# The end of the attention in a hybrid block: two modulation tiles, four norms and the first row of the output projection written earlier

## The chip, the cores and the metric

The kernel runs on one core of a Trainium2 chip. The metric is device time in microseconds (us); the median of several runs counts. A core has five engines with queues of their own: TensorE (PE: matmuls and transposes into PSUM), VectorE (DVE), ScalarE (ACT), GpSimd (POOL) and SyncE (SP), which here only issues DMA transfers. Each engine takes its instructions in the order in which they are queued.

## What is computed (the reference, cut)

One layer of a diffusion backbone: 512 latent tokens of width 2048 and 256 context tokens that serve only as extra keys and values.

```python
mod_l = silu(c) @ w_ada + b_ada            # 6 x 2048 modulation values
sh_a, sc_a, gt_a, sh_f, sc_f, gt_f = split(mod_l, 6)
h = rms_norm(x, g_mix_norm) * (1 + sc_a) + sh_a
qa, kva, kr, cb, cc, ch = split_projection(h @ w_in)
att  = softmax(q @ k.T * scale) @ v        # 8 heads of 128, keys: latent + context
conv = cb * (dwconv3(cc * ch) + bias)      # 8 groups of 128
mix  = rms_norm per group of 128 of [att, conv]
x = x + gt_a * (mix @ w_out)
x = x + gt_f * conv_ffn(rms_norm(x) * (1 + sc_f) + sh_f)
return rms_norm(x, g_final)
```

The change lies between `softmax(...) @ v` and `mix @ w_out`.

## The kernel before, in words

Arrays lie with features on the 128 partitions and tokens along the free axis, so a tile is 128x512 float32 (`t2`, a pool of 58 such tiles). A float32 product is made of three fp32r matmuls (`mm3`, L187 to L189): each operand is split into a rounded high part (a copy on ScalarE) and the rest (a subtraction on VectorE): high x high, high x low, low x high.

**The attention loop** (from L838) has 32 steps n: 8 heads with 4 blocks of 128 query tokens. Step n does the softmax of step n+1 (`softmax`, L745 and L748: the minimum `mn` on VectorE, then the exponential `p` on ScalarE), the six transposes of its own `p` (`transposes`, L761) with their split into `pth` (ScalarE, L764) and `ptl` (VectorE, L765), and the scores of step n+2 (`scores`, L730 to L734). At every even step the product of p and v for the half head that ended two steps before follows (`attend`: 18 matmuls `po`, and a copy to `o`, L777). Each eighth step sums the squares of two heads (`merge_sum`, L785 to L793: matmuls `gs`, a power on GpSimd); two steps later `merge` lays the factor out (`gb`, L299) and scales the heads (L803). The last product, `attend(7, 1)`, and the last `merge_sum(3)` come after the loop.

Between these, the loop carries other work:

- **Late modulation tiles.** 56 of the 96 rows of the modulation are made as dot products on VectorE: `late_load` (L145 on SyncE's queue, 1 MB into one of two buffers `raw`) brings a tile `ra`, and `late_dot(0)` and `late_dot(1)` (L263, 128x1024 each) multiply it, one step after the load. `keep` pins each L263 behind the VectorE instruction that is traced just before it. In the projection the tiles are called `ada` and have four half buffers of their own; their room is that of the attention's `p`, `pth` and `ptl` tiles.
- **Late norms.** `late_bg` holds the norms of the 8 convolution groups (`gn_apply`: four transposes `gb<-io,gn` at L299, then L374 on VectorE). Four are done before the loop, the other four in steps 25, 27, 29 and 31.
- **First weights of the output projection.** In steps 29 and 30 two loads `ofr` (768 KB each, L145) bring the weights of rows 0 to 3, into the same two `raw` buffers.

**The output projection** first makes 6 of its 16 output tiles at once: 16 rows k, each with 6 x 3 = 18 matmuls `of<-mx..` (`out_row`), for the convolution groups (k = 0 to 7) and then the heads (k = 8 to 15). `out_row` first splits its operand (`mx`, L337 and L338); the weights are split by `blocks` (`ofw`, L166 and L167, three splits of 128x512 for two rows). Rows 0 to 3 (`OUT_EARLY`) are written inside the attention's pools, the others after them, with `late_both` (two L263 and the next load) behind each row. Then come the other ten output tiles (`whole`), of which the last two are made in halves of 256 tokens (`ol0`, `ol1`), the residual (L980), the norm's sum of squares (`rms_steps`, tile `rs`) and the feed-forward part, which begins with matmuls `uf`.

**What sets the order.** Tile's scheduler orders each engine's queue: it takes what is ready first in its own estimate, and among that what stands first in the program. So a program line that moves changes a priority; only `keep` and `issue_after` force an order, and the latter only on the engine of the instruction that it names.

**PSUM** has eight banks of 128x512. In the attention, scores and other tiles share a pool; after it, `bank_of(i)` names banks, and `in_turn` deals them out. Before the change the last product and sum get banks 6 and 7, and the six output tiles banks 0 to 5.

Of the kernel before, what the change touches and what calls it, by code (L numbers as in the profile page):

```python
# [10 lines left out]
F32 = mybir.dt.float32  # L11
F32R = mybir.dt.float32r
AF = mybir.ActivationFunctionType
ALU = mybir.AluOpType
# [7 lines left out]
NK = D // P  # L22
# [9 lines left out]
G = 6  # L32
# [5 lines left out]
OUT_EARLY = 4  # L38
# [34 lines left out]
def block_kernel(ctx, tc, xt, ctxt, ctxn, c, c_ctx, w_ada, small, w_in, w_inc, w_q, w_kv, w_out,  # L73
# [3 lines left out]
    V, A, G_, PE, SP = nc.vector, nc.scalar, nc.gpsimd, nc.tensor, nc.sync  # L77
# [29 lines left out]
    one_bank = [None]  # L107
# [92 lines left out]
    bg, post, late_bg = deque(), [], []  # L200
# [70 lines left out]
    def late_load(ld):  # L271
        if late["t"] < late["end"]:
            late["raw"] = ld(late["t"])

    def late_both(ld=None):
        late_dot(0)
        late_dot(1)
        if ld is not None:
            late_load(ld)
# [120 lines left out]
    with ExitStack() as pa:  # L400
# [163 lines left out]
        for ci, (k0, n) in enumerate(zip(K0, KCH)):  # L564

            pss = first_banks(f"pf{ci}")
# [22 lines left out]
            for i, m in enumerate(ORDER[G:]):  # L589
                if i % per == 0:  # L590
                    k = min(per, len(ORDER) - G - i) * n
# [46 lines left out]
    with ExitStack() as pb:  # L638
# [112 lines left out]
        def transposes(st, pt):  # L751
            hd, tt = st
            half, b = tt // 2, tt % 2
            if b == 0:
                PT[hd, half] = [a_sb.tile([P, 6, 256], F32R, tag=f"pt{z}", bufs=2, name=f"pt{z}{hd}{half}") for z in "hl"]
            pth, ptl = PT[hd, half]
            bs = slice(b * P, (b + 1) * P)
            for u in range(2):
                tr = sml(f"t{hd}{tt}{u}")
                for kb in range(3):  # L760
                    PE.transpose(tr[:, kb * P:(kb + 1) * P], pt[:, (3 * u + kb) * P:(3 * u + kb + 1) * P], ident)  # L761
                trv = tr[:, :384].rearrange("p (k t) -> p k t", k=3)
                hi = pth[:, 3 * u:3 * u + 3, bs]
                A.copy(out=hi, in_=trv)  # L764
                V.tensor_tensor(out=ptl[:, 3 * u:3 * u + 3, bs], in0=trv, in1=hi.bitcast(F32), op=ALU.subtract)  # L765

        def attend(hd, half):
            pr, i = hd // 2, hd % 2
            pth, ptl = PT[hd, half]
            if half == 0:  # L770
                oo[hd] = t2([P, T], F32, f"o{hd}")
            po = sml(f"po{hd}{half}")
            for kb in range(6):
                c0 = (kb % 2) * 256 + i * P
                vh, vl = VV[pr, kb // 2]
                mm3(po[:, :256], (vh[:, c0:c0 + P], vl[:, c0:c0 + P]), (pth[:, kb], ptl[:, kb]), kb == 0, kb == 5)
            A.copy(out=oo[hd][:, half * 256:(half + 1) * 256], in_=po[:, :256])  # L777

        def merge_sum(pr):


            ps = sml(f"gs{pr}")
            for i in range(2):
                sq = tmp([P, T], F32, f"gq{pr}{i}")
                A.activation(sq, oo[2 * pr + i], AF.Square)  # L785
                for g in range(4):
                    PE.matmul(ps[:, i * 4 + g:i * 4 + g + 1], sq[:, g * P:(g + 1) * P], ones[:, 0:1], start=True, stop=True)
            d = den[pr]
            r = tiny(8, f"gr{pr}")
            V.tensor_tensor(out=d, in0=d, in1=d, op=ALU.mult)  # L790
            V.tensor_scalar(d, d, scalar1=EPS, scalar2=None, op0=ALU.mult)
            V.scalar_tensor_tensor(out=r, in0=ps[:, :8], scalar=1.0 / P, in1=d, op0=ALU.mult, op1=ALU.add)  # L792
            G_.tensor_tensor(out=r, in0=r, in1=half, op=ALU.pow)  # L793
            den[pr] = r

        def merge(pr):
            r = den[pr]
            for i in range(2):
                hd = 2 * pr + i
                pb_ = sml(f"gb{hd}")  # L800
                spread(pb_, r[:, 4 * i:4 * i + 4])
                o = oo[hd]
                V.scalar_tensor_tensor(out=o, in0=o, scalar=s("g_out", hd), in1=pb_, op0=ALU.mult, op1=ALU.mult)  # L803
                mixa[hd] = o
# [33 lines left out]
        for n, st in enumerate(steps):  # L838
            pr = st[0] // 2
            if n + 1 < len(steps):  # L840
                nxt_pt = softmax(steps[n + 1], ss[(n + 1) % 2])
            transposes(st, pt)
            pt = nxt_pt
            late_dot(0)
            if n + 2 < len(steps):
                ss[n % 2] = scores(steps[n + 2])
            if n % 2 == 0 and n:
                attend(*divmod(n // 2 - 1, 2))
                if n % 8 == 0:
                    merge_sum(n // 8 - 1)  # L850
            if n % 8 == 2 and n > 8:
                merge(n // 8 - 1)
            late_dot(1)
            if n > 24 and n % 2:
                deque(late_bg[4 + (n - 25) // 2], 0)

            at = n % 8
            if at == 0 and n and n < 24:
                fetch(pr + 1, 1)
            if pr < 3 and n:  # L860
                f, p_, i = pieces(pr + 1)[at]
                f(p_, i)
            if at < 2 and n < 24:
                fetch(pr + 1, 2 + at)
            elif at >= 2 and n < 29:
                late_load(ada_raw)
                if at == 6 and n < 16:
                    fetch(pr + 2, 0)
            if n in (29, 30):
                k = 2 * (n - 29)  # L870
                out_raw[k] = load(w_out_first[k // 2], 2 * G * P, f"ofr{k}")
            pump(2)

# [3 lines left out]
        def bank_of(i, nm):  # L877
            return p8.tile([P, 512], F32, tag=f"s{i}", bufs=1, name=nm)

        def in_turn(order):  # L880

            banks = deque(order)

            def f(nm):
                banks.rotate(-1)
                return bank_of(banks[-1], nm)

            return f


        for i in range(8):
            bank_of(i, f"bank{i}")
        one_bank[0] = in_turn((6, 7))
        attend(7, 1)
        merge_sum(3)
        pss = [bank_of(g, f"of{g}") for g in range(G)]
        mix = []

        def out_row(k, w):
            mix.append(hilo((mixc + mixa)[k], T, f"mx{k}"))  # L900
            row(pss, w[k % 2], mix[k], k)

        for k in range(OUT_EARLY):
            if k % 2 == 0:
                w = row_weights(w_out_first, k, "of", raw=out_raw[k])
            out_row(k, w)
        merge(3)
        drain()


    ph0.close()
    one_bank[0] = in_turn((6, 7, 0, 1, 2, 3, 4, 5))
    f_sb = ph1.enter_context(tc.tile_pool(name="fsb", bufs=1, side="right", reuse_waits="tile"))
    spare["w"] = f_sb, 2, 3
    g_sb = ph1.enter_context(tc.tile_pool(name="gsb", bufs=1, side="right", reuse_waits="tile"))
# [72 lines left out]
    for k in range(OUT_EARLY, NK):  # L988
        if k % 2 == 0:
            w = row_weights(w_out_first, k, "of")  # L990
        out_row(k, w)
        late_both(ada_spare if k % 4 < 3 or k == NK - 1 else None)
    for m in range(NK - 2):
        x_tile(m)
        residual(m, pss[m] if m < G else whole([load(w_out[m - G], D, f"o{m}r")], mix, f"o{m}", ld=ada_spare, often=m > 9))
# [166 lines left out]
    pss = [bank_of(i, f"uf{g}") for g, i in enumerate((2, 3, 4, 5, 1, 0))]  # L1162
# [508 lines left out]
```

## Time and profile before

| | us |
|---|---|
| median of 3 runs | 2132.49 (2132.07 to 2137.19) |
| the profiled execution | 2139.37 |
| its span in the trace | 2137.6 |
| PE busy | 2091.0 |
| DVE busy | 1826.5 |
| ACT busy | 1047.5 |

The profile is of one execution. A line of a timeline gives the start, the duration, engine, line of the kernel, operation, output<-inputs, and in brackets the idle time before it with what released it. Matmuls are pipelined, so their durations overlap: the distance between starts is what one costs. A line of waits gives who waited for whom, and the total, the count and the longest. "PEclk" is the share of full clock that was granted to TensorE.

In this execution the attention's loop runs from about 447 to 619 us, the first rows of the projection begin at 628, and the projection ends near 813.

### The profile page before, as it was taken

The page shows a single profiled execution, that of the slowest core. Times are in us where ns is not written, and L with a number is a line of the kernel's source. Part 1 is how long each engine was busy: PE and PEld are TensorE (multiplying, and loading weights), DVE is VectorE, ACT ScalarE, POOL GpSimd, SP SyncE. Part 2 cuts the span into 40 slices and gives each one's busy share as a digit, 9 for nine tenths or more (in the row PEclk, how much of TensorE's full clock was granted, in tenths as well). Part 3 has the DMA queues.
Part 4 walks back from the last instruction along what each step waited for, and adds up shares of the span by engine and source line. Part 5 has one row for each costly group of instructions (what it writes and reads, how often), then busy time and mean ns, then how long its engine had stood idle before and what let it go on. Part 6 is the DMA issues. An engine that isn't in the chain of part 4 may idle for free.

```text
span 2137.6 us, 35318 instructions
## 1 busy us (share of the span) xinstructions
PE 2091.0 (98%) x13268; PEld 1881.8 (88%) x13268; DVE 1826.5 (85%) x3024; ACT 1047.5 (49%) x1715; POOL 117.2 (5%) x144
## 2 busy tenths in 40 slices
PE   7999999999999999999999999999999999999997
PEld 4688788888988888999999999999999889999997
DVE  7998987778896989898999999999999658888887
ACT  5533333555552337565555555555655433333445
POOL 0000000000000100011000000000000000000000
PEclk9999999999999999999999999999999999999999
DMA  8989886334459986577788888788888989878684
GB/s 331 343 279 329 276 275 195 126 128 152 166 188 353 348 283 220 142 217 207 230 238 232 233 233 244 224 234 234 235 229 229 362 306 307 250 231 239 197 236 134
DMA packets 170177, 513.75 MB, mean 240 GB/s; under 512 B 18963, under 2 KB 23315, under 8 KB 164371
## 3 DMA queue, kind: packets, MB, share of 16 engines
q1 hardware_dynamic: 133364, 418.14, 57.7%
q0 software_dynamic: 17408, 59.25, 14.1%
q10 hardware_dynamic: 19232, 34.09, 4.2%
q8 instruction: 104, 1.70, 0.3%
q14 instruction: 69, 0.56, 0.1%
HBM read 464.22 MB, written 46.14 MB: 239 GB/s over the span
## 4 chain that ended last, share of the span: by engine, by line
PE 90%; DVE 4%; DMA 3%; ACT 2%; issue 1%; SPq 0%; DVEq 0%; ACTq 0%; POOLq 0%
PE pp L187 4%; PE pp L189 4%; PE pp L188 4%; PE d L187 1%; PE o L187 1%; PE d L188 1%; PE o L188 1%; PE d L189 1%; PE o L189 1%; PE uf L187 1%; PE uf L189 1%; PE uf L188 1%; PE of L187 1%; PE of L188 1%; PE of L189 1%; PE pf L188 1%
## 5 line engine op out<-in xcount | busy, mean ns | idle before, releaser
L1151 POOL DMA_DIRECT2D u_s<-in_w_up x80 | 68.6, 857 | 684.0 <-DMA u_s<-in_w_up 378.1
L263 DVE SCALAR_TENSOR_TENSOR ada<-ada,sv 128x1024 f32<-128x1024 f32 x68 | 82.1, 1220 | 11.4 <-DMA ada<-in_w_ada 11.2
L166 ACT CAST w_0h<-rw 128x512 fp32r<-128x512 f32 (+1 forms) x63 | 38.3, 618 | 108.3 <-PE pp L188 67.6
L241 DVE SCALAR_TENSOR_TENSOR ada<-ada,sv 128x1024 f32<-128x1024 f32 x64 | 77.6, 1220 | 2.2 <-DMA ada<-in_w_ada 2.1
L530 DVE SCALAR_TENSOR_TENSOR ada<-ada,svc 128x1024 f32<-128x1024 f32 x64 | 76.0, 1219 | 2.5 <-DMA ada<-in_w_ada 2.4
L167 DVE TENSOR_TENSOR w_0l<-rw,w_0h 128x512 fp32r<-128x512 f32 (+1 forms) x63 | 42.7, 683 | 22.8 <-ACT w_0h L166 22.6
L263 DVE SCALAR_TENSOR_TENSOR ra<-ra,sv 128x1024 f32<-128x1024 f32 x44 | 52.5, 1219 | 1.1 <-DMA ra<-in_w_ada 1.1
L1265 DVE TENSOR_TENSOR u<-u,u_s 128x1024 f32<-128x1024 f32 x40 | 48.8, 1220 | 0.7 <-DMA u_s<-in_w_up 0.5
L1266 DVE TENSOR_TENSOR u<-u,u 128x1024 f32<-128x1024 f32 x40 | 48.7, 1218 | 0.0
L793 POOL TENSOR_TENSOR gr<-gr,half 128x8 f32<-128x8 f32 x4 | 10.1, 2524 | 630.1 <-DVE gr L792 538.2
L764 ACT CAST pth<-t 128x384 fp32r<-128x384 f32 x64 | 28.6, 485 | 26.4 <-PE t L761 26.4
L1075 DVE TENSOR_TENSOR tp<-a,tp 128x256 fp32r<-128x256 f32 x90 | 37.7, 419 | 3.3 <-ACT tp L1074 3.3
L1074 ACT CAST tp<-a 128x256 fp32r<-128x256 f32 x90 | 35.7, 403 | 5.5 <-DMA yl6h<-y_d 4.2
L1038 ACT ACTIVATE g<-g 128x512 f32<-128x512 f32 x43 | 27.3, 634 | 18.3 <-DVE g L1032 18.0
L541 DVE TENSOR_TENSOR acc<-acc,pp 128x512 f32<-128x512 f32 x50 | 34.1, 683 | 2.1 <-PE pp L189 2.1
L765 DVE TENSOR_TENSOR ptl<-t,pth 128x384 fp32r<-128x384 f32 x64 | 33.2, 550 | 2.6 <-ACT pth L764 2.6
L745 DVE TENSOR_REDUCE mn<-s 128x1 f32<-128x768 f32 x32 | 30.4, 953 | 4.9 <-PE s L734 4.6
L1030 ACT ACTIVATE g<-cg,sm 128x512 f32<-128x512 f32 x40 | 32.6, 815 | 0.0
L1030 ACT ACTIVATE a<-ca,sm 128x512 f32<-128x512 f32 x40 | 32.1, 802 | 0.0
L748 ACT ACTIVATE p<-s,mn 128x768 f32<-128x768 f32 x32 | 29.3, 916 | 1.6 <-DVE mn L745 1.3
L1031 DVE SCALAR_TENSOR_TENSOR g<-cg,sm,g 128x511 f32<-128x511 f32 x40 | 29.8, 746 | 0.0
L1032 DVE SCALAR_TENSOR_TENSOR g<-cg,sm,g 128x511 f32<-128x511 f32 x40 | 29.8, 746 | 0.0
(10238 smaller groups left out, 8925.0 us busy)
## 6 DMA issues: line engine op xcount, KB each, us to landing
ada<-in_w_ada SPq DMA_DIRECT2D x196, 512.0 KB, 5.7
u<-in_w_up SPq DMA_DIRECT2D x120, 512.0 KB, 8.9
w<-t_d SPq DMA_DIRECT2D x161, 256.0 KB, 5.3
u_s<-in_w_up SPq DMA_DIRECT2D x80, 512.0 KB, 4.0
u_s<-in_w_up POOLq DMA_DIRECT2D x80, 512.0 KB, 9.6
t_d<-tp ACTq DMA_DIRECT2D x126, 256.0 KB, 5.9
v<-in_w_dnw SPq DMA_DIRECT2D x72, 384.0 KB, 5.1
ra<-in_w_ada SPq DMA_DIRECT2D x22, 1024.0 KB, 4.8
```

Of the source, the lines that this page charges most:

```text
L166: A.copy(out=hi[:, :n], in_=raw[:, a:a + n])
L167: V.tensor_tensor(out=lo[:, :n], in0=raw[:, a:a + n], in1=hi[:, :n].bitcast(F32), op=ALU.subtract)
L187: PE.matmul(ps, w[0], x[0], start=first, stop=False, skip_group_check=on_top)
L188: PE.matmul(ps, w[0], x[1], start=False, stop=False, skip_group_check=on_top)
L189: PE.matmul(ps, w[1], x[0], start=False, stop=last, skip_group_check=on_top)
L241: V.scalar_tensor_tensor(out=r, in0=r, scalar=1.0, in1=vec[:, i * 1024:(i + 1) * 1024], op0=ALU.mult, op1=ALU.mult, accum_out=col[:, i:i + 1])
L263: keep(V.scalar_tensor_tensor(out=r, in0=r, scalar=1.0, in1=svs[i], op0=ALU.mult, op1=ALU.mult, accum_out=lc[:, t % 4:t % 4 + 1] if i else ...
L530: keep(V.scalar_tensor_tensor(out=raw[q], in0=raw[q], scalar=1.0, in1=svc[:, q * 1024:(q + 1) * 1024], op0=ALU.mult, op1=ALU.mult, accum_o ...
L1030: A.activation(u, src, AF.Identity, bias=s("fb", m), scale=s("fw", 86 + m))
L1151: G_.dma_start(r[-1], src[more], accum_op=ALU.add)
L1265: V.tensor_tensor(out=a11, in0=a11, in1=s1, op=ALU.add)
L1266: V.tensor_tensor(out=a12, in0=a12, in1=a11, op=ALU.add)
```

## The change

1. The late norms are applied in steps 24, 25, 26 and 27 in place of 25, 27, 29 and 31.
2. The last three late tiles of the loop are loaded in steps 24, 25, 26 in place of 26, 27, 28, and multiplied in steps 25, 26, 27.
3. The weights `ofr` of rows 0 to 3 are loaded in steps 27 and 28 in place of 29 and 30.
4. Row 0 of the projection is written ahead of `attend(7, 1)` and `merge_sum(3)`, which follow between row 0 and row 1.
5. The banks: the last product and sum get 0 and 1, the six output tiles 4, 5, 6, 7, 2, 3; the tiles after them follow in the turn 0, 1, 4, 5, 6, 7, 2, 3.
6. The last `ptl` is remembered, and what `late_both` traces at row 4 is queued behind it with `issue_after`.

```diff
-                V.tensor_tensor(out=ptl[:, 3 * u:3 * u + 3, bs], in0=trv, in1=hi.bitcast(F32), op=ALU.subtract)
+                ptl_last[:] = [V.tensor_tensor(out=ptl[:, 3 * u:3 * u + 3, bs], in0=trv, in1=hi.bitcast(F32), op=ALU.subtract).ins]
+
+        ptl_last = []
...
-            if n > 24 and n % 2:
-                deque(late_bg[4 + (n - 25) // 2], 0)
+            if 24 <= n < 28:
+                deque(late_bg[4 + n - 24], 0)
...
-            elif at >= 2 and n < 29:
+            elif (at >= 2 or n >= 24) and n < 27:
                 late_load(ada_raw)
...
-            if n in (29, 30):
-                k = 2 * (n - 29)
+            if n in (27, 28):
+                k = 2 * (n - 27)
                 out_raw[k] = load(w_out_first[k // 2], 2 * G * P, f"ofr{k}")
...
-        one_bank[0] = in_turn((6, 7))
-        attend(7, 1)
-        merge_sum(3)
-        pss = [bank_of(g, f"of{g}") for g in range(G)]
+        one_bank[0] = in_turn((0, 1))
+        pss = [bank_of(b, f"of{b}") for b in (4, 5, 6, 7, 2, 3)]
...
             out_row(k, w)
+            if k == 0:
+                attend(7, 1)
+                merge_sum(3)
...
-    one_bank[0] = in_turn((6, 7, 0, 1, 2, 3, 4, 5))
+    one_bank[0] = in_turn((0, 1, 4, 5, 6, 7, 2, 3))
...
-        late_both(ada_spare if k % 4 < 3 or k == NK - 1 else None)
+        with tc.issue_after(ptl_last[0]) if k == OUT_EARLY else ExitStack():
+            late_both(ada_spare if k % 4 < 3 or k == NK - 1 else None)
```

## The prediction

> **What bounds the kernel now.** I read the page first (engine shares, chain of waits), then busy time by windows around the change, then the list of what TensorE waited for, then the timelines of TensorE, VectorE and SyncE's DMA queue over the same 40 us.
>
> ```profile
> span 2137.6 us, 35318 instructions
> ...
> PE 90%; DVE 4%; DMA 3%; ACT 2%; issue 1%; SPq 0%; DVEq 0%; ACTq 0%; POOLq 0%
> ```
>
> TensorE carries nine tenths of the chain that ended last, so a microsecond taken out of its waits is, at first, a microsecond of the span. In the windows the columns are the stretch, its length, busy time of PE, PEld, DVE, ACT, POOL, then granted clock, DMA share and GB/s:
>
> ```profile
> 590.00:607.00 17.00, 17.00 (x131) 16.02 (x130) 12.81 (x22) 7.32 (x16) 2.48 (x1) 1.00 0.37 133
> 607.00:620.00 13.00, 10.94 (x84) 9.74 (x82) 13.00 (x25) 8.04 (x20) 0.00 (x0) 1.00 0.28 90
> 620.00:632.00 12.00, 9.68 (x35) 8.66 (x36) 12.00 (x23) 10.38 (x21) 0.00 (x0) 0.57 0.68 239
> ...
> 640.00:695.00 55.00, 55.00 (x243) 44.70 (x242) 35.69 (x64) 12.76 (x22) 0.67 (x1) 1.00 0.95 351
> ```
>
> Up to 607 TensorE is full. From 607 to 632 VectorE is full, TensorE is not, and between 620 and 632 its granted clock is 0.57. From 632 TensorE is full again. So the place where this change can gain is these 25 us. What TensorE waited for there (us in total, times, longest):
>
> ```profile
> PE po L187 <- DVE den L791: 1.5, 1, 1.5
> PE po L188 <- DVE ptl L765: 1.4, 1, 1.4
> PE t L761 <- DVE ptl L765: 1.0, 1, 1.0
> PE s L730 <- ACT p L748: 0.4, 1, 0.4
> PE po L187 <- ACT p L748: 0.2, 1, 0.2
> ```
>
> That is 4.5 us of idle, nearly all of it behind VectorE's low parts `ptl`. The slow clock comes on top:
>
> ```profile
> 616.18 0.28 PE L188 MATMUL po<-ptl,v30h 128*128 128x256 f32 x1
> ...
> 618.22 0.82 PE L761 MATMUL t<-io,p 128*128 128x128 f32 x6
> 618.87 0.62 PE L299 MATMUL gb<-io,gn 128*128 128x128 f32 x4
> ...
> 622.68 0.58 PE L188 MATMUL po<-ptl,v30h 128*128 128x256 f32 x1 [1.35 <-DVE ptl L765]
> ...
> 626.47 1.70 PE L787 MATMUL gs<-io,gq 128*128 128x1 f32 x8
> 628.03 0.77 PE L187 MATMUL of<-mx0h,ofw_0h 128*128 128x512 f32 x1
> ...
> 632.01 0.40 PE L187 MATMUL of<-mx0h,ofw_0h 128*128 128x512 f32 x1
> ...
> 634.10 0.40 PE L187 MATMUL of<-mx1h,ofw_4h 128*128 128x512 f32 x1
> 634.34 0.95 PE L787 MATMUL gs<-io,gq 128*128 128x1 f32 x8
> ```
>
> Starts are compared, since ends overlap. The same 17 matmuls of a product of p and v take 2.04 us at full clock (616.18 to 618.22) and 3.79 in the last product (622.68 to 626.47): 1.75 lost. Eight sums of squares take 1.70 (626.47) against 0.95 (634.34): 0.75. The first nine matmuls of row 0 take 3.98 (628.03 to 632.01), its other nine 2.09 (632.01 to 634.10): 1.89. Together 4.4 us, and with the idle 4.5 there are **8.9 us to win**.
>
> **The two modulation tiles and two norms.** Loads of steps 26, 27, 28 become those of 24, 25, 26; each is multiplied (two instructions of L263) one step later. The norms (L374, with four transposes each) of steps 25, 27, 29, 31 go to 24 to 27. Nothing disappears: four L263 and two L374 leave the full stretch after 608 and enter the one before it.
>
> ```profile
> 595.00:608.00 13.00, 13.00 (x101) 12.24 (x101) 9.03 (x15) 5.99 (x14) 2.48 (x1) 1.00 0.24 87
> ```
>
> ```profile
> 601.20 1.02 DVE L765 TENSOR_TENSOR ptl<-t,pth 128x384 fp32r<-128x384 f32 x2
> ...
> 615.10 0.74 DVE L374 SCALAR_TENSOR_TENSOR acc<-acc,sm,gb 128x512 f32<-128x512 f32 x1
> ...
> 619.13 1.22 DVE L263 SCALAR_TENSOR_TENSOR ra<-ra,sv 128x1024 f32<-128x1024 f32 x1
> ...
> 620.27 0.55 DVE L765 TENSOR_TENSOR ptl<-t,pth 128x384 fp32r<-128x384 f32 x1
> ...
> 622.07 1.02 DVE L765 TENSOR_TENSOR ptl<-t,pth 128x384 fp32r<-128x384 f32 x2
> ```
>
> One L263 holds VectorE for 1.14 us (619.13 to 620.27), an L374 about 0.7: 4 x 1.14 + 2 x 0.7 = 6.0 us enter a stretch in which VectorE is idle for 13.00 - 9.03 = 4.0. When their data is there decides how much fits:
>
> ```profile
> 591.07 0.33 SPq L145 DMA_DIRECT2D ra<-in_w_ada  x1
> 601.31 0.33 SPq L145 DMA_DIRECT2D ra<-in_w_ada  x1
> 618.02 9.04 SPq L145 DMA_DIRECT2D ofr<-in_w_out_first  x3
> 627.11 0.90 SPq L145 DMA_DIRECT2D ada<-in_w_ada  x2
> ...
> DMA to landing us min/median/max: 4.3/4.7/7.7
> ```
>
> The loads already go out when one of the two raw buffers comes free, at 591.07 and 601.31, steps before their use; the moved tiles take these slots and land at 595.8 and 606.0. The first tile's two L263 and the norms (3.7 us) fit into the idle 4.0. The second tile's two cannot start before 606.0: 2.3 us run over, and TensorE, which needs `mn` and `ptl` queued behind them on VectorE, comes that much later to step 28. The ends are 0 (idle of the steps before 595 takes the rest) and 6.0 (none of the idle is used); I take **2.3**, the landing row being the nearest. The two norms' transposes (0.62 for the four of one, at 618.87) leave TensorE's stretch after 608 for a full one before; at nothing, and at most 1.2 gained if the run-over covers them.
>
> **Row weights, two steps earlier.** On SyncE's queue they stand behind the tiles' loads. The buffer of step 25's tile is free at 606.0 + 2.3 = 608.3 against 618.02; the shortest landing of the row, 4.3, puts the first at 612.6 (the longest at 616.0), the second, behind the third tile's L263, an estimated 3 us on. The three splits (0.6 each on ScalarE, which is idle for 5 us of 607 to 620, then VectorE) are done by about 617. POOL's queue is not passed: its power for heads 4 and 5 stays in step 24.
>
> **Row 0 ahead of the last product.** The last transposes end now at 618.22 + 0.82 = 619.0; without the 1.6 us of waits before them and with the 2.3 they end at 619.7. Row 0 is 18 matmuls at 2.09 / 9, so 4.2 us, to 623.9. The last `ptl` (now ready at 623.1) no longer stands behind the L263 that ended at 620.27 nor L374, and is ready under this cover; without the cover the old 1.5 + 1.4 come back. The product then ends near 626.0, against 626.5 now, with row 0 already done. With no gap over about 1 us the clock should stay up, so the 4.4 go too. Behind row 0 in TensorE's queue now stand the last product, the sums of heads 6 and 7 and POOL's power; they are wanted only by rows 14 and 15.
>
> Here the Trainium skill (TensorE: Matmul & The Clock Gate, Part 1) differs: it says the clock is halved after an idle window of about 3.4 us and returned after about 3.4 us of sustained work. The trace shows TensorE without a gap from 622.68 and slow until 632.01, 9.3 us. By the page's 3.4 us the clock would have been back at 626.1, only 1.75 would be clock loss, and the sum below would be 4.0 in place of 6.6 (2128.5). The measurement decides, so that outcome gets 0.02 below.
>
> **At nothing.** The guard at row 4 orders VectorE instructions of its block behind the last `ptl`; after step 27 no tile is pending, so the block holds two loads on SyncE's queue and no VectorE instruction. The new order of PSUM banks puts the sum of squares of the first half (`rs`) into the bank of output tile 14:
>
> ```profile
> 806.60 0.28 PE L316 MATMUL rs<-io,fq0t 128*128 128x1 f32 x2
> ```
>
> ```profile
> 806.70 0.48 DVE L980 SCALAR_TENSOR_TENSOR x<-ol,mod,x 128x256 f32<-128x256 f32 x1
> ```
>
> ```profile
> 811.54 0.37 ACT L327 COPY rl<-rs 128x256 f32<-128x256 f32 x1 [2.33 <-PE rs L299]
> ```
>
> ```profile
> 805.66 5.52 DMA ada<-in_w_ada
> ...
> 812.82 0.48 DVE x L980
> ```
>
> ```profile
> DVE ada L263 <- DMA ada<-in_w_ada: 10.4, 8, 2.9
> ```
>
> It must wait for the read that ends at 807.2, 0.6 later. Its result is laid out by 811.9 and used only behind the residual that ends at 813.3; that hides 0.6. Uncovered it costs 0.6.
>
> **Sum.** 8.9 - 2.3 = 6.6 us. The profiled run took 2139.37 (span 2137.6), 6.9 above the median and longer than all three timed runs; I take that difference as constant: 2132.8 for such a run, **2125.9** for the median. With the ends of the overrun (0 to 6.0) the case runs from 2123.6 to 2129.6.
>
> **Rivals.** (1) *The weight stream takes it back.* The modulation loads of the projection start at 627.11, right behind the product that frees their room; that product ends only 0.5 us earlier. The projection moves data at a DMA share of 0.95, and its end hangs on a landing (805.66 + 5.52, then the residual at 812.82). If this stream set the pace, the gain is 0.5 to 2, say 1: 2131.5. Against it: VectorE waited only 10.4 us in 185 for these landings, and TensorE never. (2) *Row 0 does not get ahead.* Four of its six banks last held transposes and the product before. The waits' first row shows the last product's first matmul, whose operand came from ScalarE, held for VectorE: for its bank. If row 0 waits for the last `ptl` like that, the cover is gone: 6.6 - 2.9 = 3.7, 2128.8. The Trainium skill (PSUM — Partial Sum Buffer, PSUM bank collisions raise a hardware error) has it that two engines must not touch a bank at once; the trace agrees as far as that 1.5 us wait shows. (3) *Slower.* In step 26 VectorE meets the second tile's L263 right behind the `ptl` that ends at 601.20 + 1.02, with `mn` and the next `ptl` queued after it, and sits from 602.2 to the landing at 606.0: 3.8 us that TensorE, fed by those, loses. A gap like that of 619.0 to 622.68 then drops the clock again for 4.4: 8.9 - 2.3 - 3.8 - 4.4 = -1.6, so 2134.1; with the longest landing (7.7, not 4.7) 2137.1; where the clock falls twice, 4.4 more. It decides when the gap reaches about 3 us. For it: VectorE runs in order, and that stretch becomes its fullest. Against: 591.07 was early enough by far.
>
> **How the numbers follow.** 0.3% is 6.4 us, about what a measurement of this kernel can tell from no change. The likeliest case has 0.66, and six parts in ten of it lie beyond 6.4, since its sum does and the 1.2 of the transposes can only add: 0.41 faster, 0.25 within. Rival 1 has 0.11, rival 2 0.08, the quick clock 0.02, all within. Rival 3 has 0.13, half of it with the clock falling twice. So faster 0.41, same 0.49, slower 0.10 (0.03 of it, taken from same, for what I have not seen). The range runs from 2122.5 (the 8.9 in full and most of the 1.2) to 2136.0, which leaves out the long landings and the second fall of rival 3.
>
> **What would show it.** Right: row 0's `of` matmuls between the last transposes and the last `po`; granted clock 1.00 through 620 to 632; row weights issued near 608 to 612; VectorE full from 606; the projection's last matmul 5 to 8 us earlier. Wrong: L263 waiting for its load around 603 to 609, `of` waiting for `ptl`, a clock below 0.9 anywhere from 600 to 635, or the residual of tile 15 not earlier though row 1 is.

## The result, and the profile after

The changed kernel takes 2138.82 us (median of 19 runs, 2135.49 to 2143.67) against 2134.65 for the kernel before beside it (19 runs, 2130.24 to 2139.27): a ratio of 1.0021, 95% interval 1.0012 to 1.0029, so about 4 us slower where 6.6 us faster was forecast. Its profiled execution took 2138.39 (span 2136.6) and is a usual one. The profiled execution of the kernel before, 2139.37, was not: it lies above all of its 19 timed runs. A second profile of the same kernel before (the run `c0_before` below: 2132.76, span 2131.0) is therefore the better thing to compare with, and I use it from here on.

First the windows of the changed kernel, the same columns as in the prediction:

```profile
607.00:620.00 13.00, 9.88 (x64) 8.94 (x65) 12.30 (x24) 8.39 (x19) 0.00 (x0) 0.89 0.54 184
620.00:632.00 12.00, 10.48 (x64) 9.24 (x64) 10.21 (x19) 10.25 (x21) 0.00 (x0) 0.98 0.08 20
632.00:640.00 8.00, 8.00 (x40) 6.64 (x39) 6.75 (x12) 1.88 (x3) 0.83 (x1) 1.00 0.98 352
```

The clock between 620 and 632 is 0.98 where it was 0.57, as forecast. But it is 0.89 in the window before. TensorE is no fuller over the two windows (busy for 20.4 us where it was 20.6), and one number is new: the DMA share of 620 to 632 is 0.08 where it was 0.68. What TensorE waited for in the changed kernel (its three longest rows of 600 to 645), and its timeline:

```profile
PE t L761 <- ACT o L779: 2.3, 1, 2.3
PE of L187 <- DVE ptl L765: 1.5, 1, 1.5
PE t L761 <- DVE o L805: 1.2, 1, 1.2
```

```profile
606.98 0.55 PE L761 MATMUL t<-io,p 128*128 128x128 f32 x3 [1.21 <-DVE o L805]
...
610.85 0.82 PE L761 MATMUL t<-io,p 128*128 128x128 f32 x6
...
616.45 1.55 PE L761 MATMUL t<-io,p 128*128 128x128 f32 x9 [2.31 <-ACT o L779]
617.65 0.56 PE L187 MATMUL po<-pth,v30h 128*128 128x256 f32 x1
...
620.57 0.29 PE L188 MATMUL po<-ptl,v32h 128*128 128x256 f32 x1
...
623.51 0.50 PE L187 MATMUL of<-mx0h,ofw_0h 128*128 128x512 f32 x1 [1.51 <-DVE ptl L765]
...
627.81 0.28 PE L187 MATMUL po<-pth,v30h 128*128 128x256 f32 x1
...
629.97 0.95 PE L789 MATMUL gs<-io,gq 128*128 128x1 f32 x8
```

Row 0 stands where it was meant to, between the last transposes and the last product. But it waits 1.51 us for the very `ptl` that it was to cover, the product before it now has the slow clock (0.21 a matmul from 617.65 to 620.57), and the last product ends at 629.97 where the prediction had 626.0. The 1.21 and the 2.31 us are new. In the first, the transposes at 606.98 wait for L805, and on VectorE a multiplication L263 now stands ahead of that:

```profile
605.04 1.22 DVE L263 SCALAR_TENSOR_TENSOR ra<-ra,sv 128x1024 f32<-128x1024 f32 x1
...
606.18 1.40 DVE L805 SCALAR_TENSOR_TENSOR o<-o,sm,gb 128x512 f32<-128x512 f32 x2
```

In the second, the transposes wait for ScalarE's copy of a product, by the look of it for the bank that the copy reads. ScalarE's own timeline shows why the copy is late:

```profile
612.82 0.62 ACT L166 CAST ofw_0h<-ofr 128x512 fp32r<-128x512 f32 x1 [3.88 <-DMA ofr<-in_w_out_first]
613.35 0.62 ACT L166 CAST ofw_4h<-ofr 128x512 fp32r<-128x512 f32 x1
613.87 0.61 ACT L166 CAST ofw_8h<-ofr 128x512 fp32r<-128x512 f32 x1
...
616.02 0.38 ACT L779 COPY o<-po 128x256 f32<-128x256 f32 x1
```

The moved row weights land at 612.8, as worked out, and their three splits now stand ahead of a `pth`, an exponential and that copy. ScalarE takes its queue in order and waited 3.88 us for the landing, although the transposes for that `pth` had ended at 611.67 (610.85 + 0.82). From 600 to 632 TensorE is idle for 5.9 us in the changed kernel and for 4.4 in `c0_before`.

The size of the loss is not there, though. Row 2 starts at 635.1 in the changed kernel and at 635.8 in `c0_before`, row 4, with all sums of squares done in both, at 645.1 and 644.9, the first matmul of output tile 14 at 784.6 and 784.4, and the first matmul of the up projection, which ends this part, at 817.0 and 813.1. From tile 14 to the up projection it is 32.4 us against 28.7. The chain of waits there, of the changed kernel:

```profile
801.65 5.62 DMA ada<-in_w_ada
...
811.61 0.60 DVE ada L263
...
812.85 3.24 DMA ufr<-in_w_up_first
816.11 0.84 ACT ufw0h L1027
817.00 0.58 PE uf L187
```

and of `c0_before`:

```profile
802.70 5.71 DMA ada<-in_w_ada
808.51 1.25 DVE ada L263 x2
...
813.07 0.58 PE uf L187
```

Both end on the stream of modulation tiles (`ada`, 68 loads in four rooms, each multiplied by L263). In the changed kernel its last multiplication starts at 811.61 and not 808.51. The weights of the up projection are queued on SyncE behind the stream's loads; in the changed kernel the first of them also waits until that last multiplication is done (812.85, in `c0_before` 806.30). This adds little, since ScalarE waits for their landing for 0.23 us. How the stream fell behind shows at its start. SyncE's queue in the changed kernel:

```profile
608.75 7.54 SPq L145 DMA_DIRECT2D ofr<-in_w_out_first  x3
630.16 5.15 SPq L145 DMA_DIRECT2D ada<-in_w_ada  x5
635.58 0.33 SPq L145 DMA_DIRECT2D ofr<-in_w_out_first  x1
```

and in `c0_before`:

```profile
617.29 9.04 SPq L145 DMA_DIRECT2D ofr<-in_w_out_first  x3
626.38 12.43 SPq L145 DMA_DIRECT2D ada<-in_w_ada  x8
639.08 0.33 SPq L145 DMA_DIRECT2D ofr<-in_w_out_first  x1
```

Two things differ. The first load goes out at 630.16, not 626.38: its room is that of the last product's operands, and the product is later. And ahead of the next row weights (rows 6 and 7) stand 5 loads, not 8. Counted on along the queue, 48 loads stand ahead of the weights of output tile 14 where there were 50. What is behind in loads is behind in VectorE's work: busy time of L263 alone in the last two stages (columns: stretch, length, VectorE busy, clock, DMA share, GB/s), changed kernel and then `c0_before`:

```profile
784.00:800.00 16.00, 6.62 (x12) 1.00 0.68 240
800.00:815.00 15.00, 7.27 (x12) 0.89 0.68 218
```

```profile
784.00:800.00 16.00, 5.86 (x11) 1.00 0.73 246
800.00:815.00 15.00, 5.46 (x10) 0.84 0.86 291
```

13.9 us of it are left at 784 where 11.3 were left before: 2.6 more, about two of its instructions at 1.2 each.

### The profile page after: what moved, and what is told of

It is laid out like the page before. It is cut to its first block, busy times and chain, and to the rows that moved or that the text cites. A ratio compares the mean times of both kernels' runs of the same rounds, so it can differ in the third digit from the quotient of the medians.

```text
span 2136.6 us, 35303 instructions
## 1 busy us (share of the span) xinstructions
PE 2086.7 (98%) x13268; PEld 1876.4 (88%) x13268; DVE 1825.4 (85%) x3024; ACT 1047.8 (49%) x1715; POOL 117.0 (5%) x144
## 4 chain that ended last, share of the span: by engine, by line
PE 89%; DMA 4%; DVE 4%; ACT 2%; issue 1%; SPq 0%; DVEq 0%; ACTq 0%; POOLq 0%
PE pp L187 4%; PE pp L189 4%; PE pp L188 4%; PE d L187 1%; PE d L188 1%; PE d L189 1%; PE o L187 1%; PE o L188 1%; PE o L189 1%; PE uf L187 1%; DMA ada<-in_w_ada 1%; PE uf L188 1%; PE uf L189 1%; PE of L187 1%; PE of L188 1%; PE of L189 1%
## 5 line engine op out<-in xcount | busy, mean ns | idle before, releaser
L263 DVE SCALAR_TENSOR_TENSOR ada<-ada,sv 128x1024 f32<-128x1024 f32 x68 | 82.3, 1220 | 10.4 <-DMA ada<-in_w_ada 10.2
L263 DVE SCALAR_TENSOR_TENSOR ra<-ra,sv 128x1024 f32<-128x1024 f32 x44 | 52.4, 1216 | 1.0 <-DMA ra<-in_w_ada 1.0
L795 POOL TENSOR_TENSOR gr<-gr,half 128x8 f32<-128x8 f32 x4 | 10.2, 2542 | 631.2 <-DVE gr L794 584.7
L761 PE MATMUL t<-io,p 128*128 128x128 f32 x192 | 28.1, 275 | 3.5 <-ACT o L779 2.3
L1035 DVE SCALAR_TENSOR_TENSOR g<-cg,sm,g 128x511 f32<-128x511 f32 x40 | 29.8, 745 | 0.0
```

Of the source, the lines that this page charges most:

```text
L263: keep(V.scalar_tensor_tensor(out=r, in0=r, scalar=1.0, in1=svs[i], op0=ALU.mult, op1=ALU.mult, accum_out=lc[:, t % 4:t % 4 + 1] if i else ...
```

## The experiments

Each was timed beside the kernel before. "The stretch" is the time from the first matmul of output tile 14 to the first of the up projection in the run's profiled execution; "ahead" is the number of modulation loads on SyncE's queue ahead of the weights of rows 6 and 7, and of output tile 14. The profiled executions of `e2_row0_only` and `f4_two_rows` are the slowest of theirs (2144.49 and 2146.34), so their stretch says more of the order than of the median.

| run | rows ahead of the product | ahead | stretch, us | median, us | ratio to before (95%) |
|---|---|---|---|---|---|
| c0_before | 0 | 8, 50 | 784.4 to 813.1: 28.7 | 2133.49 | 0.9996 (0.9986 to 1.0005) |
| e1_moves_only | 0 | 9, 50 | 784.1 to 812.6: 28.5 | 2135.81 | 1.0003 (0.9993 to 1.0013) |
| f3_banks_only | 0 | 8, 50 | 786.3 to 815.7: 29.4 | 2136.51 | 1.0007 (0.9998 to 1.0016) |
| f2_before_room | 0 | 8, 50 | 785.6 to 814.1: 28.5 | 2135.10 | 0.9997 (0.9988 to 1.0007) |
| the change | 1 | 5, 48 | 784.6 to 817.0: 32.4 | 2138.82 | 1.0021 (1.0012 to 1.0029) |
| e2_row0_only | 1 | 5, 48 | 786.7 to 819.9: 33.2 | 2141.11 | 1.0022 (1.0011 to 1.0033) |
| e3_rs_bank | 1 | 5, 48 | 785.4 to 819.9: 34.5 | 2140.07 | 1.0020 (1.0009 to 1.0031) |
| f1_after_room | 1 | 5, 48 | 788.7 to 822.4: 33.7 | 2142.69 | 1.0032 (1.0021 to 1.0044) |
| g1_after_early | 1 | 5, 48 | 786.1 to 819.8: 33.7 | 2140.61 | 1.0029 (1.0018 to 1.0039) |
| f4_two_rows | 2 | 0, 46 | 788.2 to 824.5: 36.3 | 2140.88 | 1.0028 (1.0017 to 1.0040) |
| i1_before_order | 0 | 4, 48 | 785.2 to 818.0: 32.8 | 2139.97 | 1.0026 (1.0014 to 1.0037) |
| h2_after_order | 1 | 8, 50 | 794.6 to 827.6: 33.0 | 2149.10 | 1.0066 (1.0049 to 1.0083) |
| h4_after_lead | 1 | 12, 57 | 813.9 to 840.5: 26.6 | 2160.74 | 1.0111 (1.0089 to 1.0133) |
| j1_early_and_order | 1 | 8, 50 | 794.2 to 821.7: 27.5 | 2144.95 | 1.0061 (1.0043 to 1.0079) |
| j2_moves_early_lead | 0 | 9, 51 | 786.5 to 813.2: 26.7 | 2135.29 | 1.0004 (0.9992 to 1.0017) |

**The parts.** My first theory (A) was that the stream takes the gain back and the bank of `rs` adds to it; B said that the new banks cost everything; C that the moved work overloads VectorE. The guard at row 4 needs no experiment: without it the queues of all five engines are the same.

`c0_before`, the kernel before, unchanged:

> The kernel before itself, unchanged, for a second profile and as a measure of the noise. All theories: ratio 1.000 within 0.1%. Its profiled run should lie near 2134.7 us, some 4 us below the profiled run of before (2139.4), and show in which stage that one lost them.

`e1_moves_only`, without row 0's move and the banks:

```diff
-            if n > 24 and n % 2:
-                deque(late_bg[4 + (n - 25) // 2], 0)
+            if 24 <= n < 28:
+                deque(late_bg[4 + n - 24], 0)
-            elif at >= 2 and n < 29:
+            elif (at >= 2 or n >= 24) and n < 27:
-            if n in (29, 30):
-                k = 2 * (n - 29)
+            if n in (27, 28):
+                k = 2 * (n - 27)
```

> Only the norms, the two modulation tiles and the row weights are moved (steps 24 to 28); row 0 stays behind the last product and the PSUM banks stay as before. Theory A (the stream of modulation loads sets the end of the projection and takes back what the attention's end gains; the later rest is the bank of the sum of squares): row 2 of the projection starts 1 to 3 us earlier than 639.2, the last output tile's weights land no earlier than 790, time within 0.1% of before. Theory B (the new banks cost everything): faster than before by 2 to 4 us, since the banks are old. Theory C (the moved work overloads VectorE in steps 24 to 27): slower by 3 to 5 us, as the whole change is.

`e2_row0_only`, row 0's move and the banks alone:

```diff
+        one_bank[0] = in_turn((0, 1))
+        pss = [bank_of(b, f"of{b}") for b in (4, 5, 6, 7, 2, 3)]
...
+            if k == 0:
+                attend(7, 1)
+                merge_sum(3)
...
+    one_bank[0] = in_turn((0, 1, 4, 5, 6, 7, 2, 3))
```

> Only row 0 is written ahead of the last product, with the new PSUM banks; norms, modulation tiles and row weights stay in their old steps. Theory A: row 2 starts 1 to 3 us earlier, the end of the projection no earlier, the sum of squares 1 to 2 us later because of its bank: slower than before by 1 to 3 us. Theory B: slower by about 4 us, as the whole change is. Theory C: as before, within 0.1%.

`e3_rs_bank`, the whole change with the bank of `rs` taken elsewhere:

```diff
-        one_bank[0] = in_turn([6 * h])
+        one_bank[0] = in_turn([6 + h])
```

> The whole change, but the sums of squares of the two halves get banks 6 and 7, free since output tiles 10 and 11, in place of bank 0 (still output tile 14's) and 6. Theory A: the sum of squares starts at about 806.6 again and not 808.6, the time falls by 1 to 2 us from the whole change's, not below the kernel before. Theory B: it falls by 4 us or more, to the kernel before or below it. Theory C: no difference from the whole change.

The moves cost and bring nothing that can be measured, row 0 with the banks carries the whole loss (1.0022, the change 1.0021), and the bank of `rs` is not it. So C falls, and A's second half.

**The start of the stream, or the banks?** Theory D: the stream has a length of its own and starts when the last product frees its room. Theory E: the turn of the banks. Theory F: the order at the projection's end.

`f1_after_room`, the whole change, and `f2_before_room`, the kernel before, each with the operands of the last product laid lower:

```diff
+        for z in ("h1", "l1", "h0", "l0"):
+            a_sb.tile([P, 6, 256], F32R, tag=f"pt{z}", bufs=1, name=f"lay{z}")
...
-                PT[hd, half] = [a_sb.tile([P, 6, 256], F32R, tag=f"pt{z}", bufs=2, name=f"pt{z}{hd}{half}") for z in "hl"]
+                PT[hd, half] = [a_sb.tile([P, 6, 256], F32R, tag=f"pt{z}{half}", bufs=1, name=f"pt{z}{hd}{half}") for z in "hl"]
```

> The whole change, with one thing beside it: the operand tiles of the last product (half 1 of each head) lie at the low end of the attention's room, so that three of the four rooms of the projection's modulation tiles and all of the spare weight room lie under tiles that are read earlier than the last product. Theory D (the stream of modulation loads through four rooms runs at a pace of its own, about 175 us from the first of its 68 loads to the last, and starts when the last product frees its room; row 0 ahead of the product starts it at 630.2 in place of 626.4): the first load goes out right behind the row weights, before 620, the stream ends about 10 us sooner, the first matmul of the up projection starts at 806 to 811 (817.0 in the changed kernel) and the time is 2127 to 2133. Theory E (the new turn of the PSUM banks costs what was lost): nothing is touched that matters, 2138 to 2140. Theory F (the queues' order at the projection's end costs it, not the start of the stream): 2137 to 2141, with the first load early all the same.

> The kernel before with the same new layout of the last product's operand tiles and nothing else. D: its stream too waits for the last product (first load at 626.4 to 627.1), only less; it starts 5 to 8 us sooner, the up projection at 808 to 812 (813.1 to 815.8), time 2128 to 2133 against 2134.7. E and F: 2134.7, no difference that can be measured.

`f3_banks_only`, the kernel before with the three lists of banks:

```diff
-        one_bank[0] = in_turn((6, 7))
+        one_bank[0] = in_turn((0, 1))
-        pss = [bank_of(g, f"of{g}") for g in range(G)]
+        pss = [bank_of(b, f"of{b}") for b in (4, 5, 6, 7, 2, 3)]
-    one_bank[0] = in_turn((6, 7, 0, 1, 2, 3, 4, 5))
+    one_bank[0] = in_turn((0, 1, 4, 5, 6, 7, 2, 3))
```

> The kernel before with the three new lists of PSUM banks alone; row 0 stays behind the last product. D: the stream starts at 626 to 627 as before, time 2133 to 2136, the same as before. E: the banks carry the loss, 2138 to 2141.

`f4_two_rows`, rows 0 and 1 ahead:

```diff
-            if k == 0:
+            if k == 1:
                 attend(7, 1)
```

> The whole change with rows 0 and 1 ahead of the last product in place of row 0 alone: the suspected delay doubled. D: the first modulation load goes out another 3.8 to 4.2 us later, near 634, the up projection starts at about 821 and the time is 2142 to 2144. E: the banks are those of the change, 2138 to 2140. F: no more than 1 us from the changed kernel.

The banks alone cost 1.0007 (0.9998 to 1.0016), which can't be told from nothing and is not the loss of the change, so E falls. Two rows ahead lengthen the stretch to 36.3, with no load ahead of the weights of rows 6 and 7 and the first load at 638.0; the time, 1.0028, can't be told from that of the change. The room runs did not do what I meant: the room of the very first load still reached 1.5 KB (in each partition) into the last product's tile, and the other loads stand behind it in the queue, so the first went out at 634.1 and 627.7. They decide nothing, except that the stretch did not shrink.

**The date of the first load, or the order of the queue?** Theory G: what costs is the order, 5 and 48 for 8 and 50.

`g1_after_early`, `f1_after_room` with the two pools swapped, so that the first four loads touch nothing of the last product:

```diff
-    f_sb = ph1.enter_context(tc.tile_pool(name="fsb", bufs=1, side="right", reuse_waits="tile"))
-    spare["w"] = f_sb, 2, 3
     g_sb = ph1.enter_context(tc.tile_pool(name="gsb", bufs=1, side="right", reuse_waits="tile"))
+    f_sb = ph1.enter_context(tc.tile_pool(name="fsb", bufs=1, side="right", reuse_waits="tile"))
+    spare["w"] = f_sb, 2, 3
```

> The whole change, the last product's operands laid low as in the run before, and the rooms of the modulation tiles laid above the spare weight room, so that this time the first four loads of the stream touch nothing that the last product reads; the first waits for the product before it. The queues keep the changed kernel's order. Theory D (the loss is the late start of the stream): first load 620 to 626, first matmul of the up projection at 806 to 812, time 2128 to 2133. Theory G (the loss is the order of the queues: row 0 ahead frees weight rooms for one row earlier, so that the weights of rows 6 and 7 are queued behind 5 modulation loads in place of 8, the load of output tile 14 behind 48 in place of 50, and the last loads and dots come after it): first load early all the same, first matmul of the up projection at 815 to 820, time 2137 to 2141.

Its queue, and pieces of the end of its chain:

```profile
622.75 13.20 SPq L145 DMA_DIRECT2D ada<-in_w_ada  x5
636.23 0.33 SPq L145 DMA_DIRECT2D ofr<-in_w_out_first  x1
```

```profile
804.65 8.41 DMA ada<-in_w_ada
...
813.16 1.22 DVE ada L263
...
819.83 0.58 PE uf L187
```

The first load is out 7.4 us sooner than in the change, and nothing is won: D falls. The chain still ends on the stream, although the weights of the up projection go out at 809.07 here and are not waited for.

`i1_before_order`, the kernel before with each modulation load held behind the row weights written before it (`fetched` remembers the load that was written last):

```diff
+        fetched[:] = [ins.ins]
...
             w = row_weights(w_out_first, k, "of")
+            row_load = fetched[0]
         out_row(k, w)
-        late_both(ada_spare if k % 4 < 3 or k == NK - 1 else None)
+        late_dot(0)
+        late_dot(1)
+        if k % 4 < 3 or k == NK - 1:
+            with tc.issue_after(row_load):
+                late_load(ada_spare)
```

> The kernel before, with row 0 behind the last product and the old banks; only the modulation loads written after the weights of a later pair of rows are held behind that load on SyncE's queue, which gives nearly the changed kernel's order (4, 6, 10 and, for output tile 14, 48 modulation loads ahead of the weights, against 8, 12, 14 and 50). Theory D: the first load goes out at 626 to 627 as before, time 2133 to 2136. Theory G: the loss of the change without its row 0: first matmul of the up projection at 816 to 820, time 2137 to 2141.

Its queue, and pieces of the end of its chain:

```profile
624.42 2.48 SPq L145 DMA_DIRECT2D ada<-in_w_ada  x4
637.13 0.33 SPq L145 DMA_DIRECT2D ofr<-in_w_out_first  x1
```

```profile
813.97 3.16 DMA ufr<-in_w_up_first
...
817.15 0.84 ACT ufw0h L1029
...
818.03 0.58 PE uf L188
```

With row 0 behind, the old banks and the first load as early as ever, the order by itself makes the loss: 5.3 us, the stretch 32.8, and the same late `ufr` (813.97, in the change 812.85). Its profiled execution has a long slow clock at the attention's end (619.1 to 629.3), but tile 14 starts at 785.2 all the same, 0.8 later than in `c0_before`.

**Undoing it.** `h2_after_order` writes two tiles ahead of row 4 and holds later row weights behind the load written last; `h4_after_lead` does it with four; neither has the guard:

```diff
+        if k == OUT_EARLY:
+            for j in range(2):
+                late_both(ada_spare)
         if k % 2 == 0:
-            w = row_weights(w_out_first, k, "of")
+            with tc.issue_after(fetched[0]) if k > OUT_EARLY else ExitStack():
+                w = row_weights(w_out_first, k, "of")
```

> The whole change (without the guard at row 4, which orders nothing) with two modulation tiles written ahead of row 4 and the weights of each later pair of rows held behind the modulation load written last: 8, 10, 14 loads ahead of the weights of rows 6, 8, 10 and 50 ahead of output tile 14, which is the order before; the late loads of output tile 15 stand behind 64 in place of 60. Theory D: the first load goes out at 630 as in the changed kernel, time 2138 to 2140. Theory G: most of the loss comes back: first matmul of the up projection at 811 to 815, time 2132 to 2136.

> The same with four tiles ahead of row 4 in place of two: 12, 14, 18 loads ahead of the weights of rows 6, 8, 10 and 57 ahead of output tile 14, all 68 ahead of output tile 15. Theory G: the stream ends before the last two output tiles, the first matmul of the up projection comes at 805 to 810 and the time is 2126 to 2132, below both kernels, unless row 6 waits for its weights behind twelve loads; where it waits (up to 8 us) 2134 to 2140. Theory D: 2138 to 2140.

`j1_early_and_order` is `g1_after_early` with the hold of `h2_after_order` and its two tiles ahead of row 4, and with two tiles passed over at tile 13, which puts the weights of tile 15 back behind 60 loads; `j2_moves_early_lead` is `e1_moves_only` with the rooms of `g1_after_early`, the same hold and one tile ahead of row 4.

> The whole change (without the guard that orders nothing) with both repairs at once: the rooms laid so that the first loads wait for the product before the last, and the weights of later pairs of rows held behind 8, 10, 14 modulation loads and those of output tile 14 behind 50, output tile 15's behind 60 as before. Theory G in its second form (the order costs the loss, and an order as before can only be had where the loads may also start early, else the rows wait for weights as they did with the order alone): no wait of the rows for weights, first matmul of the up projection at 811 to 815, time 2132 to 2136. Theory H (row 0 ahead of the product costs what was lost in another way, at the projection's end): 2138 to 2141, with the rows free of waits.

> The moved tiles, norms and row weights with row 0 behind the last product and the old banks, the rooms laid for early loads, and one modulation tile written ahead of row 4 with the same hold: 9, 12, 14 and, for output tile 14, 51 loads ahead. Theory G: at the time of the kernel before or a little below, first matmul of the up projection at 808 to 814, 2130 to 2135. If holding the weights costs by itself: rows wait for weights, 2136 to 2142.

What TensorE waited for, of `h2_after_order`, `h4_after_lead` and `j1_early_and_order`:

```profile
PE of L188 <- ACT ofw_0h L167: 6.2, 2, 4.1
PE ol L188 <- ACT o150w0h L167: 4.0, 1, 4.0
```

```profile
PE of L188 <- ACT ofw_0h L167: 22.4, 1, 22.4
```

```profile
PE of L188 <- ACT ofw_0h L167: 6.4, 2, 5.2
```

The hold moves the loss instead of removing it. Where the stream is brought forward by force the stretch does fall (27.5 with the old order, 26.6 with four tiles ahead), but rows 6 and later wait for their weights, and tile 14 starts 10 us late (794.6 and 794.2) or 29 (813.9). In `h2_after_order` tile 15 stood behind 64 loads and waited 4.0 itself. My expectations G for all three were wrong in the sum, since they had the rows' price at nothing or as an aside. `j2_moves_early_lead` has the short stretch without such a wait (26.7), but starts tile 14 at 786.5, and its time can't be told from that of the kernel before.

**The stream made shorter.** `k1_after_two_less` and `k2_before_two_less` take the last two of the 34 modulation tiles off the stream, in the change and in the kernel before: they leave out the loads and products of these two, and set their columns of the modulation to zero. The queues are otherwise the same up to tile 15.

```diff
-    late = {"t": 32, "raw": None, "end": 88}
+    late = {"t": 32, "raw": None, "end": 86}
+    V.memset(mod[:, 86:88], 0.0)
```

> The changed kernel with the last two of the 34 modulation tiles of the projection left out (tiles 86 and 87: neither loaded nor multiplied, their columns of the modulation set to zero); the order of all queues is the changed kernel's up to output tile 15, only four loads and four dots at the end are gone. Theory G (the loss is that two loads more, and their dots, stand behind the load of output tile 14, so that the stream and not TensorE ends the projection): without them the stretch from the first matmul of output tile 14 to the first of the up projection falls from 32.4 us to 27 to 29, the first matmul of the up projection comes at 811 to 814, time 2132 to 2136. Theory H (row 0 ahead of the product costs in another way): that stretch stays above 31, time 2137 to 2140.

> The kernel before with the same two modulation tiles left out. Theory G: it has less to gain, since its stream ended nearly with TensorE: the same stretch falls from 28.7 us to 26 to 28, time 2131 to 2134.5, and the changed kernel without them comes within 2 us of it (4 to 5 with all tiles). Theory H: the distance stays at 4 to 5.

The stretch falls as G had it, from 32.4 to 28.4 (789.0 to 817.4) in the change, and from 28.7 to 26.9 (787.5 to 814.4) in the kernel before; 3.7 us of distance become 1.5. The up projection itself begins at 817.4 where G had 811 to 814, because tile 14 starts 4.4 us later in this profile than in that of the change. The times are 2136.58 (ratio 1.0008, 0.9998 to 1.0018) and 2132.03 (0.9989, 0.9980 to 0.9997). The ratios are 0.0019 apart with an uncertainty of some 0.0013, so between 1 and 7 us are left between the two where G had under 2: this pair doesn't settle whether the lag is all of the loss.

## Why the prediction was wrong

In short: what row 0 pushes back was taken to be "wanted only by rows 14 and 15". The runs show that row 0 ahead of the product changes the order of the loads, and that this order costs 3.7 us at the projection's end. The stall that was to pay for the change was smaller than read, and part of it came back in other waits.

**"8.9 us to win" came from an odd execution.** The idle 4.5 us are in `c0_before` too (4.4). Most of the slow clock is not. Its TensorE timeline:

```profile
621.95 0.39 PE L188 MATMUL po<-ptl,v30h 128*128 128x256 f32 x1 [1.35 <-DVE ptl L765]
...
626.42 0.48 PE L187 MATMUL of<-mx0h,ofw_0h 128*128 128x512 f32 x1
...
630.69 0.40 PE L187 MATMUL of<-mx1h,ofw_4h 128*128 128x512 f32 x1
```

Its granted clock is 0.50 from 622.5 to 626.0, for 3.4 us, and row 0 then runs at full speed (18 matmuls in 630.69 - 626.42 = 4.27 us, 6.07 in the profile that I worked from). From the product's second matmul to the first of row 1 it is 8.74 us (621.95 to 630.69), and 11.42 in that profile (622.68 to 634.10): 2.7 of the 4.4 are gone, and the 6.6 is 3.9 at most. The 2132.49 that I subtracted from was the median of usual runs; the stall that I subtracted was that of an unusual one. I saw that the profiled run was 6.9 above the median and called the difference constant: it sat partly in the stretch that I was costing. The outcome that I gave 0.02 priced the gain at 4.0, near those 3.9; its side was wrong too. The Trainium skill (TensorE: Matmul & The Clock Gate, Part 1) returns the clock after about 3.4 us of work. The 3.4 here agrees with it, the profile that I worked from does not.

**"The run-over 2.3" was the wrong cost of the moved work.** No L263 waited for its load. But on VectorE one of them stands ahead of L805, and TensorE waits 1.21 us there, in a row that `c0_before` doesn't have. The larger wait, 2.31 us, came from the row weights' splits on ScalarE. I had those splits at nothing, covered by 5 us in which ScalarE was idle, and didn't name what stands behind them in its queue, nor that a queue whose head waits for a landing is no cover. That 2.31 agrees with my 2.3 is an accident. `e1_moves_only` has both waits (1.21 and 2.38) and 5.9 us of idle time in all, 1.5 more than `c0_before`; its clock is 1.00 from 600 to 632, and row 2 comes at 635.5, 0.3 before the 635.8 of `c0_before`. The moves took away the slow clock of that stretch and put waits of about the same size in its place.

**"Row 0 covers the wait for the last `ptl`" failed as rival 2 had it.** Row 0 waits 1.51 us for that `ptl`, and the last transposes end later than forecast. The product ends at 629.97 instead of 626.0.

**"Wanted only by rows 14 and 15" was the step that lost the time.** Row 0 ahead of the product was costed as free for everything behind it. Two rows of the prediction spoke against that: the modulation loads start "right behind the product that frees their room", and the projection's end "hangs on a landing". I used both in rival 1 and let the product come out 0.5 us earlier, so that the stream could only give less gain back, never more than the gain. What the trace shows is a queue in another order: 5 loads ahead of the next row weights in place of 8, kept to the end as 48 for 50, and 3.7 us more from tile 14 to the up projection. That this order suffices for the loss, without row 0 ahead and without the new banks, is shown by `i1_before_order`. That a late first load, the bank of `rs` and the moved work are not needed for it is shown by `g1_after_early`, `e3_rs_bank` and `e2_row0_only`; that neither the moves nor the banks make it alone, by `e1_moves_only` and `f3_banks_only`. The stretch goes with the order: 28.5 to 29.4 us with 50 loads ahead of tile 14 (the four kernels in which no load is held), 32.4 to 34.5 with 48 (six kernels), 36.3 with 46 (one), so some 2 us for a load. Why the order changes is only seen as a series (8, 5 and 0 loads ahead with no, one and two rows ahead) and argued: a row written ahead is planned to free its weight rooms sooner, so that the next weights are queued sooner. That the lag is the whole of it stays open, since neither `j1_early_and_order` nor the pair without two tiles brought the times together. Behind the first matmul of the up projection the profiles differ by as much as the loss and show no side: 1319.6 us in the change, 1317.9 in `c0_before`, 1321.8 in the other profile of the kernel before.

**The rest.** The guard costs nothing, as said. The bank of `rs` at "0.6, hidden" holds too: taking it away changed nothing. The sign that I named for being wrong, the projection's end not earlier though row 1 is, is what came beside the profile that I worked from: its row 1 starts at 634.10, that of the change at 630.78, and the up projection at 815.8 and 817.0. (Beside `c0_before`, with row 1 at 630.69, not even row 1 is earlier.) Rival 3 had the right side for another reason; no L263 waited in step 26.

## What to carry to other kernels

Profile the kernel before twice when the gain is a stall of a few us: a clock stretch of one execution is not the price of the others. When a step is moved ahead of another in a program whose queues are planned, compare the order of every queue behind it, and count what stands ahead of the stream that the next stage ends on. Here a stream that fell behind at its start (5 loads for 8) was still behind 150 us later (48 for 50), where nothing covered it. And when loads move earlier, ask what stands in the queue behind the instruction that waits for their landing.

## What the runs showed of the hardware

At the end of the attention and at the end of the projection the slow clock lasts one or several times the same 3.4 us, and the granted share is 0.50. Around the end of the attention it lasts 3.4 us in fourteen of the eighteen profiles (617.2 to 620.6 in the change, 622.5 to 626.0 in `c0_before`), 10.2 us, three times as long, in two (621.8 to 632.0 in the profile of the prediction, 619.1 to 629.3 in `i1_before_order`), and does not occur in two (`e1_moves_only`, `j2_moves_early_lead`). At the end of the projection it lasts 3.4, 6.8, 10.2 or 13.7 us. Windows of `c0_before`, of the profile of the prediction and of `e1_moves_only`, the columns as in the prediction:

```profile
622.50:626.00 3.50, 3.50 (x20) 3.50 (x18) 3.50 (x7) 3.38 (x8) 0.00 (x0) 0.51 0.18 72
```

```profile
622.00:632.00 10.00, 9.32 (x34) 8.47 (x35) 10.00 (x18) 8.75 (x17) 0.00 (x0) 0.50 0.59 207
```

```profile
600.00:632.00 32.00, 26.09 (x180) 22.85 (x179) 29.91 (x56) 20.86 (x45) 2.48 (x1) 1.00 0.57 194
```

The first two are executions of one kernel. The length of the wait before does not decide it: `e1_moves_only` waited 2.38 us and kept its clock, the change waited 2.31 and lost it. No run tells what decides.
